# First-stage weight tiles requested two ahead, normed rows of the recurrence requested in two parts, modulation tiles and o-gate blocks at other places

## The chip, the core and the metric

The kernel runs on one core of one Trainium2 chip. The core has five engines, each of which takes its own instructions strictly in order: TensorE (PE in the profile, with its weight loads as PEld), VectorE (DVE), ScalarE (ACT), GpSimd (POOL) and SyncE (SP), which here only issues transfers from HBM. Engines meet through semaphores: an instruction whose input isn't ready holds up everything behind it on its engine.

The metric is the device time of one execution in microseconds (us), as the median of several runs.

## What is computed

A trunk of two layers over 256 positions of width 2048, all in float32. Layer 0 has an mLSTM mixer, layer 1 a gated linear recurrence; each is followed by an MLP with a squared ReLU. Ahead of each of the four parts stands a modulated RMS norm, whose shift, scale and gate come from the vector c through a matrix of 2048 x 6144.

```python
def ada_modulate(x, c, w, b):
    mod = jax.nn.silu(c) @ w + b
    shift, scale, gate = jnp.split(mod, 3, axis=-1)
    h = rms_norm(x) * (1.0 + scale[:, None, :]) + shift[:, None, :]
    return h, gate[:, None, :]

def mlstm_mixer(h, w_in, b_gate, norm_g, w_out):
    proj = h @ w_in                      # q, k, v, o and two gates per head
    ...
    hh = mlstm_chunkwise(q, k, v, li, lf).transpose(0, 2, 1, 3)
    hh = hh * lax.rsqrt(jnp.mean(hh * hh, axis=-1, keepdims=True) + EPS)
    hh = hh.reshape(B, S, V_W) * norm_g.astype(jnp.float32)
    return (hh.astype(h.dtype) * jax.nn.sigmoid(o)) @ w_out

def rglru_mixer(h, w_in, conv_w, conv_b, w_ra, b_ra, w_ri, b_ri, lam, w_out):
    xb, gb = jnp.split(h @ w_in, 2, axis=-1)
    ...                                  # convolution over 4 positions, two gates, scan
    y = hs.astype(h.dtype) * jax.nn.gelu(gb)
    return y @ w_out

# layer 0: x += gate * mlstm(h); x += gate * mlp(h); layer 1: the same with rglru; final norm
```

## The kernel before

**Arithmetic.** Every float32 operand is split into a high and a low part, and a product is made of two or three matmuls. A weight tile of 128 x 2048 (1 MB) arrives as `raw` (four buffers, tag "raw"); `weights()` (lines 158 to 170) requests it on SP's queue (L160) and cuts it into two halves, `whi` on ACT (L167) and `wlo` on DVE (L168), with four buffers of each, so two tiles' worth. An activation row of 128 x 256 is split into a `pair` (ACT L180 or L177, DVE L181 or L178).

**Modulation tiles.** The matrix of the modulations comes as 192 tiles of 1 MB (`adaraw`, requested at L124), each of which DVE multiplies and sums in one instruction (L126). They belong to no particular place: `fill()`, `pace()` and `need()` (lines 134 to 150) lay them down between the weight tiles, at rates set by `QKV_RATE` (per weight tile in the five groups of the first stage) and by `PACE` (how many are to be done by the end of each later stage).

**First stage** (`group()`, lines 472 to 525). The 16 rows of 128 inputs are normed in five groups of 2, 4, 4, 4 and 2; forty weight tiles cover q, k, v and half of the o columns. For each weight tile, `group()` requests it, splits it, and multiplies it into accumulators `mm` in PSUM (L498); groups after the first preload the accumulator with the sum so far (ACT L513), and each accumulator is copied out again (ACT L524). After 34 tiles and the direct first one, and before the last group of five, stands the gate block (`gblk`, L550), which has a weight tile of its own.

**Heads and o-gate blocks** (`mix0`, lines 545 to 755). Eight heads follow, each with scores, state, numerator and denominator (`num`, `den`), mean square (`hss`) and gating. The other half of the o columns is computed in eight o-gate blocks, one weight tile each, that stand between the steps of the heads; the tuple `OB` says where. Its first entry stands ahead of the first scores, entries 1 + 2h and 2 + 2h behind the state and behind the scores of the next head. After every second head two normed, gated rows of `th` are made and split into `zhi` (ACT L718) and `zlo` (DVE L719). The output projection then takes one quad of blocks and twelve single blocks, each of which ends in `residual()` (xall, L329).

**Recurrence** (lines 760 to 864). For n = 0 and 1 the products run on rows that aren't normed yet (`unnormed`) and are corrected afterwards; from n = 2 (`MORE_RG`) on they use the 16 normed rows, made by `modulated()` from `hmod` (DVE L304) and `pair` (ACT L180, DVE L181). All 16 are asked for at n = 2 (lines 796 and 797). Gate products (`gacc`) of each n follow its convolution (`xf`, DVE L805 and L808).

The order on each engine is written out by a scheduler from the program's order, priorities (splits and modulation sums are brought forward) and buffers, so that edits to the program shift rows of several engines.

Of the kernel before, what the change touches and what calls it, by code (L numbers as in the profile page):

```python
# [8 lines left out]
F32 = mybir.dt.float32  # L9
# [6 lines left out]
P = 128  # L16
DM = 2048
S = 256
KC = DM // P
# [22 lines left out]
MORE_RG = 2  # L42
# [6 lines left out]
GROUPS = (2, 4, 4, 4, 2)  # L49
DIRECT = (0,)  # L50
OG = 8

OB = (0, 1, 0, 1, 0, 1, 0, 1, 0, 1, 0, 1, 0, 1, 0, 1, 0)

QKV_RATE = (1.6, 1, 1, 1, 1.2)
PACE = dict(o=54, out0=66, w1a=82, w1b=92, mlp0=168, mix1=170, out1=176, mlp1=192)


@with_exitstack
def trunk_kernel(ctx, tc, xT_d, par_d, ada_d, wqkv_d, wg_d, wo_d, awoa_d, awo_d, bwi_d, bg_d, bwo_d,  # L60
                 w1a_d, w1b_d, bwia_d, w1_d, w2_d, out_d):
    nc = tc.nc
# [5 lines left out]
    wpool = ctx.enter_context(tc.tile_pool(name="wpool", bufs=4))  # L68
# [86 lines left out]
        filler += [(i, 32 + j) for j in range(KC)]  # L155


    def weights(src):
        raw = wpool.tile([P, DM], F32, name="raw", tag="raw")
        nc.sync.dma_start(out=raw, in_=src)  # L160
        out = []
        for i in range(2):
            sl = raw[:, i * HALF:(i + 1) * HALF]
            hi = wpool.tile([P, HALF], F32R, name="whi", tag="whi", bufs=SPLIT_BUFS)
            lo = wpool.tile([P, HALF], F32R, name="wlo", tag="wlo", bufs=SPLIT_BUFS)
            with tc.high_priority(offset=PRIO):
                A.activation(hi, sl, AF.Copy)  # L167
                V.tensor_tensor(out=lo, in0=sl, in1=hi.bitcast(F32), op=ALU.subtract)  # L168
            out.append((hi, lo))
        return out  # L170
# [281 lines left out]
    r = tmp.tile([P, S], F32, name="nrstd", bufs=1)  # L452
    rsqrt(r, ss, 1.0 / DM, EPS)
    hs = []
# [5 lines left out]
    def group_h(gi):  # L460
# [8 lines left out]
            hs.append(p)  # L469
        return h32  # L470

    def group(gi, h32):


        gn, k0 = GROUPS[gi], sum(GROUPS[:gi])
        per = (4096 + OG * P) // 512
        nt = per * k0 // 4
        width = DM // gn
        for nb in range(per * gn // 4):
            direct = nt in DIRECT  # L480
            gh = h32 if direct else [[p[:, 0, :], p[:, 1, :]] for p in hs[k0:k0 + gn]]
            if direct:
                w = wpool.tile([P, DM], F32, name="wdir", tag="raw")
                nc.sync.dma_start(out=w, in_=wqkv_d[nt])
            else:
                w = weights(wqkv_d[nt])
            nt += 1

            def part(kk, o, n):
# [55 lines left out]
    with ExitStack() as mctx:  # L545
# [198 lines left out]
        for kg in range(4):  # L744
            w = weights(awoa_d[kg])
            for kk in range(4):
                hi, lo = w[kk // 2]
                for b in range(4):
                    o = kk % 2 * 512 + b * P
# [10 lines left out]
    with ExitStack() as mctx:  # L760
# [18 lines left out]
        hs = []  # L779
        for n4 in range(4):  # L780
# [5 lines left out]
            for n in range(n4 * 2, n4 * 2 + 2):  # L786
# [6 lines left out]
                    V.tensor_tensor(out=lo, in0=src, in1=hi.bitcast(F32), op=ALU.subtract)  # L793
                    gw.append((hi, lo))
                xf, xp = [], []
                if n == MORE_RG:
                    hs += [modulated(2, j, r) for j in range(KC)]
                for j in (2 * n, 2 * n + 1):
                    if n < MORE_RG:
                        acc, c = scaled(accs[j] if n == 0 else early_block(bwi_d[j], us), r)  # L800
# [13 lines left out]
                for d in range(2):  # L814
                    j = 2 * n + d
# [132 lines left out]
```

## Time and profile before

| | |
|---|---|
| Time, median of 3 runs | 2271.15 us (2270.98 to 2273.05) |
| The profiled execution's own time | 2271.59 us |
| Its span in the profile | 2269.9 us |
| Granted clock of TensorE, mean over the span | 0.99 |
| Read from HBM | 596.93 MB |

A profile is of one execution. Its views: busy time by engine over the span or over chosen windows; groups of instructions by line with the idle time before them; waits (which line of which engine waited for which other); the order in time of each engine's instructions; and transfers. In the rows of the order in time, the first number is the start in us, the second the length, and brackets hold the idle time before it and what released it; "x4" is four instructions in one row. A matmul's listed length reaches past the start of the next one, since they are pipelined. L-numbers are lines of the kernel before.

### The profile page before, as it was taken

The numbers are of one execution on the slowest core, as the hardware profiler recorded it, in microseconds if no ns is written. First come the engines' busy times: TensorE is split into PE (matmuls) and PEld (weight loads), VectorE is DVE, ScalarE is ACT, GpSimd is POOL, SyncE is SP. The second block draws the span as 40 slices with busy tenths as digits, with TensorE's granted clock in tenths as the row PEclk, the third lists the DMA queues.
The fourth block names the chain that finished last, engine by engine and source line by source line (L and its number), as shares of the span: only waits on it lengthen the run. The fifth ranks groups of instructions, "written<-read, shape, count | busy, mean of one in ns | idle before, by whom it ended". The sixth has DMA issues, their size and how long they took to land.

```text
span 2269.9 us, 34176 instructions
## 1 busy us (share of the span) xinstructions
PE 2191.2 (97%) x13606; PEld 1955.9 (86%) x13606; DVE 1719.1 (76%) x2199; ACT 1279.8 (56%) x1997; POOL 84.4 (4%) x70
## 2 busy tenths in 40 slices
PE   7999899999999999999999799999999999999998
PEld 6787799898888888888889799889888888888887
DVE  6777778999998778888888877898875555555554
ACT  5666687445674335555444777756664334665443
POOL 0000000210000000000110000020000000000110
PEclk9999999999999999999999899999999999999999
DMA  8988876989779989898887354676875555555552
GB/s 341 349 315 319 319 263 222 333 305 344 285 288 345 333 327 340 323 336 327 326 327 277 143 195 178 241 260 237 320 277 205 187 187 189 192 191 186 186 186 93
DMA packets 88672, 601.27 MB, mean 265 GB/s; under 512 B 10424, under 2 KB 14648, under 8 KB 16192
## 3 DMA queue, kind: packets, MB, share of 16 engines
q1 hardware_dynamic: 86400, 598.03, 72.5%
q8 instruction: 107, 1.75, 0.3%
q10 hardware_dynamic: 2112, 1.05, 0.2%
q14 instruction: 53, 0.43, 0.0%
HBM read 596.93 MB, written 2.11 MB: 264 GB/s over the span
## 4 chain that ended last, share of the span: by engine, by line
PE 73%; DVE 3%; ACT 1%; issue 1%; DVEq 0%; ACTq 0%
PE mm L193 42%; PE mm L194 22%; PE mm L211 1%; PE mm L210 1%; PE mm L212 1%; PE mm L188 1%; PE mm L187 1%; PE mm L189 1%; DVE wlo L168 1%; DVE adaraw L126 1%; PE mm L350 0%; ACT whi L167 0%; PE gacc L187 0%; PE gacc L188 0%; PE gacc L189 0%
## 5 line engine op out<-in xcount | busy, mean ns | idle before, releaser
L193 PE MATMUL mm<-pair,whi 128*128 128x512 f32 x4272 | 1497.8, 395 | 15.6 <-DVE pair L181 14.9
L194 PE MATMUL mm<-pair,wlo 128*128 128x256 f32 x4272 | 1197.2, 281 | 8.8 <-DVE wlo L168 8.8
L168 DVE TENSOR_TENSOR wlo<-raw,whi 128x1024 fp32r<-128x1024 f32 x736 | 893.7, 1234 | 375.4 <-ACT whi L167 372.0
L167 ACT ACTIVATE whi<-raw 128x1024 fp32r<-128x1024 f32 x736 | 767.2, 1056 | 568.2 <-PE mm L193 420.1
L193 PEld LDWEIGHTS mm<-pair,whi 128*128 128x128 f32 x4272 | 802.8, 188 | 203.9 <-issue 12.3
L194 PEld LDWEIGHTS mm<-pair,wlo 128*128 128x128 f32 x4272 | 804.8, 188 | 12.3 <-DVE wlo L168 11.8
L126 DVE SCALAR_TENSOR_TENSOR adaraw<-adaraw,cbc 128x2050 f32<-128x2050 f32 x192 | 438.3, 2286 | 10.9 <-DMA adaraw<-in_ada 10.7
L498 PE MATMUL mm<-pair,whi 128*128 128x256 f32 x736 | 136.3, 288 | 8.5 <-ACT mm L513 4.6
L329 DVE SCALAR_TENSOR_TENSOR xall<-mm,mod,xall 128x256 f32<-128x256 f32 x170 | 81.4, 482 | 80.3 <-PE mm L194 71.9
L498 PEld LDWEIGHTS mm<-pair,whi 128*128 128x128 f32 x736 | 114.4, 193 | 12.4 <-ACT whi L167 5.7
L188 PE MATMUL mm<-pair,whi 128*128 128x256 f32 x432 | 122.1, 283 | 0.0
L187 PE MATMUL mm<-pair,whi 128*128 128x256 f32 x432 | 121.9, 282 | 0.0
L189 PE MATMUL mm<-pair,wlo 128*128 128x256 f32 x432 | 121.6, 281 | 0.0
L498 PE MATMUL mm<-pair,wlo 128*128 128x256 f32 x368 | 104.0, 291 | 8.1 <-DVE wlo L168 7.8
L371 ACT ACTIVATE hsum<-hsum 128x256 f32<-128x256 f32 x121 | 49.4, 413 | 91.3 <-DVE hsum L254 79.3
L284 POOL TENSOR_TENSOR nacc<-nacc,nsq 128x256 f32<-128x256 f32 x52 | 74.0, 1424 | 346.4 <-ACT nsq L275 339.0
L498 PE MATMUL mm<-whi,pair 128*128 128x512 f32 x256 | 82.0, 396 | 1.0 <-ACT whi L167 0.7
L187 PEld LDWEIGHTS mm<-pair,whi 128*128 128x128 f32 x432 | 81.5, 189 | 0.4
L189 PEld LDWEIGHTS mm<-pair,wlo 128*128 128x128 f32 x432 | 81.6, 189 | 0.2 <-DVE wlo L168 0.2
L188 PEld LDWEIGHTS mm<-pair,whi 128*128 128x128 f32 x432 | 81.5, 189 | 0.0
L498 PEld LDWEIGHTS mm<-pair,wlo 128*128 128x128 f32 x368 | 70.1, 194 | 12.0 <-DVE wlo L168 12.0
L210 PE MATMUL mm<-unnormed,whi 128*128 128x258 f32 x272 | 77.4, 285 | 0.0
(217 smaller groups left out, 2038.4 us busy)
## 6 DMA issues: line engine op xcount, KB each, us to landing
raw<-in_w SPq DMA_DIRECT2D x220, 1024.0 KB, 5.0
adaraw<-in_ada SPq DMA_DIRECT2D x192, 1025.0 KB, 5.6
raw<-in_wqkv SPq DMA_DIRECT2D x39, 1024.0 KB, 7.8
raw<-in_w1a SPq DMA_DIRECT2D x32, 1024.0 KB, 6.2
raw<-in_bwi SPq DMA_DIRECT2D x28, 1024.0 KB, 4.9
raw<-in_bwo SPq DMA_DIRECT2D x16, 1024.0 KB, 4.9
raw<-in_awo SPq DMA_DIRECT2D x12, 1024.0 KB, 5.0
raw<-in_wo SPq DMA_DIRECT2D x8, 1024.0 KB, 8.6
```

The lines of the kernel that those rows point to most:

```text
L126: V.scalar_tensor_tensor(out=raw, in0=raw, scalar=1.0, in1=cbc, op0=ALU.mult, op1=ALU.mult, accum_out=mod[i][:, j:j + 1])
L167: A.activation(hi, sl, AF.Copy)
L168: V.tensor_tensor(out=lo, in0=sl, in1=hi.bitcast(F32), op=ALU.subtract)
L187: PE.matmul(out, lhsT=whi, rhs=hi, start=first, stop=False)
L188: PE.matmul(out, lhsT=whi, rhs=lo, start=False, stop=False)
L189: PE.matmul(out, lhsT=wlo, rhs=hi, start=False, stop=last)
L193: PE.matmul(out, lhsT=whi, rhs=p.rearrange("p a t -> p (a t)"), start=first, stop=False)
L194: PE.matmul(out[:, 0:S], lhsT=wlo, rhs=p[:, 0, :], start=False, stop=last)
L210: PE.matmul(out[:, 0:UX], lhsT=whi, rhs=u[:, 0:UX], start=first, stop=False)
L284: G.tensor_tensor(out=self.acc, in0=self.acc, in1=sq, op=ALU.add)
L329: V.scalar_tensor_tensor(out=xT[j], in0=acc[:, a:a + S], scalar=mod[i][:, 32 + j:33 + j], in1=xT[j], op0=ALU.mult, op1=ALU.add)
L498: PE.matmul(out, lhsT=l, rhs=m, start=clear and kk + n == 0, stop=kk == gn - 1 and n == len(ops) - 1, skip_group_check=True)
```

## The change

Weight tiles of the first stage are requested by `tile_ahead()`, which asks for tiles up to two past the one being used before that one is split; ahead of the gate block it stops at tile 34, in the last group at tile 39. The modulation rates of groups 1 to 4 fall from 1, 1, 1, 1.2 to 0.9, 0.9, 0.9, 1, and four entries of `PACE` change: 51 modulation tiles instead of 54 are done by the end of the heads, 90 instead of 92 by the end of w1b, 162 instead of 168 by the end of the first MLP and 169 instead of 170 by the end of the recurrence. One o-gate block now stands ahead of the first scores, and the one behind the state of the last head is gone. In the recurrence the normed rows 0 to 7 are asked for at n = 0 and the rows 8 to 15 at n = 1. What is computed is the same.

```diff
-OB = (0, 1, 0, 1, 0, 1, 0, 1, 0, 1, 0, 1, 0, 1, 0, 1, 0)
-
-QKV_RATE = (1.6, 1, 1, 1, 1.2)
-PACE = dict(o=54, out0=66, w1a=82, w1b=92, mlp0=168, mix1=170, out1=176, mlp1=192)
+OB = (1, 1, 0, 1, 0, 1, 0, 1, 0, 1, 0, 1, 0, 1, 0, 0, 0)
+
+QKV_RATE = (1.6, 0.9, 0.9, 0.9, 1)
+AHEAD = 2
+PACE = dict(o=51, out0=66, w1a=82, w1b=90, mlp0=162, mix1=169, out1=176, mlp1=192)
...
-    def weights(src):
+    def load(src):
         raw = wpool.tile([P, DM], F32, name="raw", tag="raw")
         nc.sync.dma_start(out=raw, in_=src)
+        return raw
+
+    def weights(src):
+        return split(load(src))
+
+    def split(raw):
         out = []
...
+    raws = []
+
+    def tile_ahead(nt, last):
+
+        while len(raws) <= min(nt + AHEAD, last):
+            raws.append(load(wqkv_d[len(raws)]))
+        return raws[nt]
+
     def group(gi, h32):
...
-            if direct:
-                w = wpool.tile([P, DM], F32, name="wdir", tag="raw")
-                nc.sync.dma_start(out=w, in_=wqkv_d[nt])
-            else:
-                w = weights(wqkv_d[nt])
+            w = tile_ahead(nt, per * (KC if gi == len(GROUPS) - 1 else KC - GROUPS[-1]) // 4 - 1)
+            if not direct:
+                w = split(w)
             nt += 1
...
-                if n == MORE_RG:
-                    hs += [modulated(2, j, r) for j in range(KC)]
+                if n < 2:
+                    hs += [modulated(2, j, r) for j in range(8 * n, 8 * n + 8)]
```

Lines move by up to 13: the split is L174 (ACT) and L175 (DVE) after, the preload L526, the copy-out L537, the modulation sum L127, hmod L311, the row's pair L187 and L188, zlo L732.

**ACT in the first stage.** The rows are in the order of ACT, around weight tiles 8 to 11. `mm<-v4` is a preload, `v0<-mm` a copy-out; qk6 and qk7 are the two accumulators of tile 8, v0 and v1 those of tile 9, v2 and v3 those of tile 10. Before, the split of tile 10 is whi_840 and whi_844:

```order
L513 ACTIVATE mm_891<-v4_199 128x512
L180 ACTIVATE pair_1108<-hmod_1106,mod0_127 128x256
L524 ACTIVATE v0_195<-mm_805 128x512
L513 ACTIVATE mm_906<-v5_200 128x512
L167 ACTIVATE whi_840<-raw_838 128x1024
L167 ACTIVATE whi_844<-raw_838 128x1024
L524 ACTIVATE v1_196<-mm_820 128x512
```

and after it is whi_841 and whi_845:

```order
L537 ACTIVATE qk6_193<-mm_739 128x512
L526 ACTIVATE mm_864<-v3_198 128x512
L174 ACTIVATE whi_841<-raw_729 128x1024
L174 ACTIVATE whi_845<-raw_729 128x1024
L537 ACTIVATE qk7_194<-mm_766 128x512
L526 ACTIVATE mm_892<-v4_199 128x512
L537 ACTIVATE v0_195<-mm_806 128x512
L526 ACTIVATE mm_907<-v5_200 128x512
L174 ACTIVATE whi_884<-raw_796 128x1024
```

Tile 10's split stood behind the copy-out of tile 9's first accumulator (v0) and now stands behind that of tile 8's first (qk6), one tile earlier. The same holds for tiles 7 to 22 and 28 to 30; the splits of tiles 23 to 27 and 31 to 34 stand as before. On PE, the products of a tile's second accumulator, which stood partly between those of its first, now follow the first for tiles 7 to 14, 16 to 22 and 28 to 31.

**DVE behind the last head.** The rows are in the order of DVE, from the mean-square part of heads 6 and 7 (rsu, rs) to their last zlo. `adaraw` is the sum of one modulation tile, `wlo` half a weight tile. Before:

```order
L126 SCALAR_TENSOR_TENSOR adaraw,mod_128<-adaraw,cbc 128x2050
L168 TENSOR_TENSOR wlo<-raw,whi 128x1024 x2
L264 SCALAR_TENSOR_TENSOR rsu<-rs,rsy 128x512
L265 SCALAR_TENSOR_TENSOR rsu<-rsu,rsy 128x512
L168 TENSOR_TENSOR wlo<-raw,whi 128x1024
L266 SCALAR_TENSOR_TENSOR rs<-rsu,rsy 128x512
L126 SCALAR_TENSOR_TENSOR adaraw,mod_128<-adaraw,cbc 128x2050
L714 TENSOR_TENSOR th<-th,rs 128x512 x2
L168 TENSOR_TENSOR wlo<-raw,whi 128x1024
L719 TENSOR_TENSOR zlo<-th,zhi 128x512
L168 TENSOR_TENSOR wlo<-raw,whi 128x1024
L719 TENSOR_TENSOR zlo<-th,zhi 128x512
```

and after:

```order
L271 SCALAR_TENSOR_TENSOR rsu<-rs,rsy 128x512
L127 SCALAR_TENSOR_TENSOR adaraw,mod_128<-adaraw,cbc 128x2050
L272 SCALAR_TENSOR_TENSOR rsu<-rsu,rsy 128x512
L127 SCALAR_TENSOR_TENSOR adaraw,mod_128<-adaraw,cbc 128x2050
L273 SCALAR_TENSOR_TENSOR rs<-rsu,rsy 128x512
L175 TENSOR_TENSOR wlo<-raw,whi 128x1024
L727 TENSOR_TENSOR th<-th,rs 128x512 x2
L127 SCALAR_TENSOR_TENSOR adaraw,mod_128<-adaraw,cbc 128x2050
L732 TENSOR_TENSOR zlo<-th,zhi 128x512
L127 SCALAR_TENSOR_TENSOR adaraw,mod_128<-adaraw,cbc 128x2050
L732 TENSOR_TENSOR zlo<-th,zhi 128x512
```

Four modulation sums now stand between the first rsu and the last zlo where one stood, and one weight half where three stood. On PE, 126 products of other blocks lay between head 7's last den and the first product that reads the zhi made from heads 6 and 7; after the change it is 69. Of the products with the first three weight tiles of the output projection's quad, 124 lay behind that den, and now 33.

**DVE in the recurrence.** The rows are in the order of DVE around the normed rows (hmod, and pair from hmod). Before, they stand behind the second convolution (gb, w and TT belong to the gates and the scan):

```order
L244 TENSOR_TENSOR gb<-mm,nrstd 128x256
L832 SCALAR_TENSOR_TENSOR w_12122<-th,xf 128x256
L246 TENSOR_SCALAR shc<-mm 128x1
L304 SCALAR_TENSOR_TENSOR hmod<-xall,mod_129,nrstd 128x256 x3
L168 TENSOR_TENSOR wlo<-raw,whi 128x1024
L304 SCALAR_TENSOR_TENSOR hmod<-xall,mod_129,nrstd 128x256 x4
```

and after, the first eight follow the norm's factor at once:

```order
L273 SCALAR_TENSOR_TENSOR nrstd<-rsu,rsy 128x256
L311 SCALAR_TENSOR_TENSOR hmod<-xall,mod_129,nrstd 128x256
L175 TENSOR_TENSOR wlo<-raw,whi 128x1024
L188 SCALAR_TENSOR_TENSOR pair<-hmod,mod_129,pair 128x256
L311 SCALAR_TENSOR_TENSOR hmod<-xall,mod_129,nrstd 128x256 x3
L175 TENSOR_TENSOR wlo<-raw,whi 128x1024
L188 SCALAR_TENSOR_TENSOR pair<-hmod,mod_129,pair 128x256 x3
L311 SCALAR_TENSOR_TENSOR hmod<-xall,mod_129,nrstd 128x256 x2
```

The other eight (hmod x1, x5 and x2, then pair x8) stand ahead of the second pair's convolution and behind its predecessor's.

## The prediction

> **What bounds the kernel now.** I read the page's busy times first, then busy time by stretch, then the waits of the stretch that loses most, then the order in time inside it. From the page:
>
> ```profile
> span 2269.9 us, 34176 instructions
> PE 2191.2 (97%) x13606; PEld 1955.9 (86%) x13606; DVE 1719.1 (76%) x2199; ACT 1279.8 (56%) x1997; POOL 84.4 (4%) x70
> raw<-in_wqkv SPq DMA_DIRECT2D x39, 1024.0 KB, 7.8
> ```
>
> TensorE (PE) is busy 97% of the span, so all edits together can win only from the 78.7 us in which it is idle, and a little more where its clock is halved. The views by window say where that idle time lies (start:end, length, PE, weight loads, DVE, ACT, POOL, clock, DMA share, GB/s):
>
> ```profile
> 25.00:85.00 60.00, 54.73 (x328) 47.75 (x328) 46.77 (x50) 37.16 (x60) 0.00 (x0) 0.94 0.91 345
> 85.00:262.00 177.00, 162.35 (x1009) 138.73 (x1009) 132.16 (x127) 113.49 (x168) 0.00 (x0) 1.00 0.87 325
> 417.00:480.00 63.00, 58.75 (x482) 58.34 (x481) 61.92 (x69) 26.77 (x44) 24.12 (x12) 0.97 0.94 348
> 440.00:480.00 40.00, 40.00 (x341) 40.00 (x340) 38.92 (x39) 16.92 (x23) 13.79 (x7) 1.00 0.99 371
> 1222.00:1273.00 51.00, 51.00 (x416) 50.21 (x415) 41.71 (x88) 36.98 (x53) 0.00 (x0) 1.00 0.59 207
> 1273.00:1286.00 13.00, 0.89 (x5) 0.61 (x4) 12.42 (x32) 11.57 (x23) 0.00 (x0) 0.58 0.22 81
> ```
>
> Two places stand out: weight tiles 8 to 34 of the first stage (85 to 262), and one hole of 12 us in the recurrence. In the first, no engine is full: DVE works 132 of 177 us. The waits there, and one tile of it in time:
>
> ```profile
> DVE wlo L168 <- ACT whi L167: 36.9, 28, 2.3
> PE mm L498 <- DVE wlo L168: 13.1, 27, 0.5
> ```
>
> ```profile
> 142.33 0.38 SPq L160 DMA_DIRECT2D raw<-in_wqkv  x1
> ...
> 148.57 0.60 ACT L524 ACTIVATE qk<-mm 128x512 f32<-128x512 f32 x1 [2.23 <-PE mm L498]
> ...
> 149.74 1.99 ACT L167 ACTIVATE whi<-raw 128x1024 fp32r<-128x1024 f32 x2
> ...
> 156.38 2.00 ACT L167 ACTIVATE whi<-raw 128x1024 fp32r<-128x1024 f32 x2
> ...
> 150.83 0.74 PE L498 MATMUL mm<-pair,whi 128*128 128x256 f32 x4 [0.18 <-ACT whi L167]
> 152.09 0.39 PE L498 MATMUL mm<-pair,wlo 128*128 128x256 f32 x1 [0.52 <-DVE wlo L168]
> 152.32 0.40 PE L498 MATMUL mm<-pair,whi 128*128 128x256 f32 x2
> ...
> 157.28 0.28 PE L498 MATMUL mm<-pair,wlo 128*128 128x256 f32 x1
> 157.48 0.73 PE L498 MATMUL mm<-whi,pair 128*128 128x512 f32 x2
> ```
>
> The tile asked for at 142.33 lands, by the page's median of 7.8 us, near 150.1, yet its split starts at 156.38. What holds it is not the transfer: the split of tile n+1 stands on ACT behind the copy-out of tile n's first accumulator (148.57 for the tile before), and ACT itself waits 2.23 us for PE there. DVE's half follows ACT's, and PE waits for both. One tile takes 157.48 − 150.83 = 6.65 us. Undisturbed, 42 products run from 152.32 to 157.28, 0.118 us each, so 48 products need 5.67. Over the stretch it is 177/27 = 6.55 us a tile: **0.88 us lost per tile**. (The busy column hides part of it, since the modelled end of each last product reaches into the gap.)
>
> **The change, part by part.** Sums are made against the profiled execution, 2271.6 us (span 2269.9 and 1.7 around it); the runs' median is 2271.15, the same within 0.02%.
>
> *Two tiles ahead.* By the ACT order, the split of tile n+2 now stands where that of n+1 stood, for tiles 8 to 22 and 28 to 30; for 23 to 27 and 31 to 34 it stands as before. Where it has moved, it is ready a whole tile early and PE should run at 5.67. Tile 31 I count with these, since PE no longer puts products of tile 30's second accumulator into its first and so frees ACT about 1 us sooner. That is 19 of the 27 tiles: 19 × 0.88 = 16.7, **+17** (gains are positive). The cover has to hold elsewhere: DVE per tile is 2 wlo (2.36), 0.9 modulation tile (0.9 × 2.37) and a pair or hmod (0.4), 4.9 of 5.67. DMA has to bring 1.9 tiles of 1.05 MB in 5.67 us, 352 GB/s, against 325 now and 371 in the densest window. From that, 325 kept means 6.13 us a tile and only +8; the other eight tiles freed as well means 27 × 0.88, +23.
>
> *Start, gate block, entry of the heads.* The first tiles' requests now go ahead of modulation tiles on SP's one queue, so the modulated rows of group 1 come later; this queue ran at 345 GB/s, and one modulation tile moved behind a raw tile is 3 us at that rate, of which PE has most covered: **−0.8**. Around the gate block the lookahead stops, so its tile is asked for as late as before, and its split stands behind one more copy-out and two modulation tiles (4.7 us) on DVE. The waits there now:
>
> ```profile
> PE mm L498 <- ACT mm L513: 4.6, 2, 3.4
> PE cp L648 <- ACT kw L630: 2.1, 1, 2.1
> ```
>
> Neither is removed; the first head's state now has one o-gate block ahead of it. Between 0 and −5, I take **−2**. The last group's lookahead reaches the end and has little left to win.
>
> *o-gate blocks and the modulation tiles.* This is where I expect the change to give back. No o-gate block is left behind the last head's state. Now:
>
> ```profile
> 390.02 0.39 PE L664 MATMUL den<-qw,Cn 128*128 128x128 f32 x2
> 391.26 0.42 DVE L668 SCALAR_TENSOR_TENSOR em<-em,ad 128x256 f32<-128x256 f32 x1
> 391.78 2.29 DVE L126 SCALAR_TENSOR_TENSOR adaraw<-adaraw,cbc 128x2050 f32<-128x2050 f32 x1
> 394.00 1.22 DVE L168 TENSOR_TENSOR wlo<-raw,whi 128x1024 fp32r<-128x1024 f32 x1
> 405.49 1.29 DVE L714 TENSOR_TENSOR th<-th,rs 128x512 f32<-128x512 f32 x2
> 406.21 0.63 ACT L718 ACTIVATE zhi<-th 128x512 fp32r<-128x512 f32 x1 [1.88 <-DVE th L714]
> 409.57 0.68 DVE L719 TENSOR_TENSOR zlo<-th,zhi 128x512 fp32r<-128x512 f32 x1
> ```
>
> From the last denominator (390.02 + 0.39 = 390.4) to the end of the first normed, gated row zhi (406.84) pass 16.4 us, since DVE puts three modulation tiles and four weight halves between. Today 126 products lie in between (14.9 us): the wait is 0.5. In the new order only 69 do (8.1 us). The DVE chain has three modulation tiles and three halves, with two more modulation tiles just ahead of it (I take 1.7 us later); zlo then has one more ahead. So PE stops for 8 to 12 us. Does out0 win it back? DVE is full from 391 to 480 (61.92 of 63 in 417 to 480), so it sets the end of out0. Behind em up to out0's end stand 16 modulation tiles and 30 halves before, 18 and 26 after: 2 × 2.37 − 4 × 1.2 = 0, the same load. But em now comes with 91 fewer products still to do (33 of the output projection's first three weight tiles instead of 124), 91 × 0.118 = 10.7 us later in PE's own work, and 1.7 more by the backlog: **−12.4**. Bounds: −5 if DVE's modulation tiles slip behind; −17 if the stop also halves the clock.
>
> That last bound needs a row of its own, taken in the recurrence:
>
> ```profile
> 1285.41 0.77 PE L193 MATMUL mm<-pair,whi 128*128 128x512 f32 x1 [12.11 <-DVE pair L181]
> ...
> 1288.11 0.63 PE L193 MATMUL mm<-pair,whi 128*128 128x512 f32 x1
> 1288.54 0.41 PE L194 MATMUL mm<-pair,wlo 128*128 128x256 f32 x1
> 1288.75 0.45 PE L193 MATMUL mm<-pair,whi 128*128 128x512 f32 x1
> ```
>
> After 12.11 us of waiting PE needs 0.64 us for a pair of products (1288.11 to 1288.75) until 3.3 us have passed: 1.7 us lost beside the wait. The Trainium skill, "TensorE: Matmul & The Clock Gate", section "What's actually happening", says the same: after an idle window of about 3.4 us the array gets half its clock until about 3.4 us of work have gone by. By that rule the new stop on the o-gate would cost 1.7 more, and the sum would be 1.7 us worse; by the DVE row for 417 to 480 that time is paid out of DVE's bound already, and I leave it out.
>
> *Recurrence.* The hole ends at 1285.41. In it DVE makes normed rows (seven of its hmod and four pairs in these groups):
>
> ```profile
> 1274.31 1.27 DVE L304 SCALAR_TENSOR_TENSOR hmod<-xall,mod,nrstd 128x256 f32<-128x256 f32 x3
> 1276.70 1.66 DVE L304 SCALAR_TENSOR_TENSOR hmod<-xall,mod,nrstd 128x256 f32<-128x256 f32 x4
> 1284.79 1.67 DVE L181 SCALAR_TENSOR_TENSOR pair<-hmod,mod,pair 128x256 fp32r<-128x256 f32 x4
> ```
>
> A row costs DVE 0.42 + 0.42, sixteen rows 13.4 us. From 1222 to 1273 DVE has 51.00 − 41.71 = 9.3 us free, and the new order puts eight rows (6.7 us) early there. The other eight stand ahead of the second pair's convolution: DVE is then 13.4 − 9.3 = 4.1 us behind, and I add 1.7 for the gate products that now find their operands late; 5.8 us of waiting remain of 12.1. With 1.7 of half clock gone: 12.1 − 5.8 + 1.7 = **+8**. Ends: +1 if DVE's free time, spent waiting for ACT's halves, can't be used; +11 if nothing remains.
>
> *Modulation tiles of the first MLP.* Four fewer stand there and five more in the recurrence, 2.37 us each on DVE, which is busy 76% of the span and has 9.3 us free in the recurrence's first part alone: 0, with ±2 for both ends.
>
> Sum: −0.8 + 17 − 2 − 12.4 + 8 = +9.8, so 2271.6 − 9.8 = **2261.8, rounded to 2262 us**.
>
> **The rivals.**
>
> 1. *The stop behind the last head stays hidden.* If DVE has run its modulation tiles ahead under the earlier o-gate blocks and isn't the bound of out0, the term is about −1. Against: DVE's own rows fill nearly all of the 16.4 us, and only 8.1 us of products lie over them. Time: 2271.6 − (9.8 + 11.4) = 2250.4.
> 2. *DMA sets the pace of the first stage.* At 325 GB/s the tile takes 6.13 us: 19 × 0.42 = 8 rather than 17, sum +0.8, 2270.8: no change. For: 0.87 share at 325 now. Against: 371 in 440 to 480, 345 from 25 to 85.
> 3. *Slower.* The same mechanism further on: a tile with 0.9 modulation tile is 1.99 MB. At 300 GB/s it needs 6.63 us, more than the 6.55 it takes now, −1.5 in all, and the sum is −8.7: 2280.3. The change turns slower by over 4.5 us when the nineteen tiles gain under 2.7 us, 0.14 each, so at 6.41 us a tile or 310 GB/s. For: requests queued two ahead compete with modulation tiles that DVE still has to free. Against: the two rows just named.
> 4. *The change doesn't do what it says.* The gap per tile stays since the split halves have no more buffers than before. Then 17 becomes 0: 2278.8. Against: in 85 to 262 ACT's split never waits for PE to free a half; it waits behind the copy-out. The Trainium skill, "Perfetto Trace Analysis", section "Optimization Strategy", speaks for it: the same gap repeating on the engine that should be saturated can mean too few buffers for the next tile. The change adds none. By the trace's order at 149.74 and 156.38 it doesn't apply.
>
> **How the numbers follow.** Forecast 0.50 (2255 to 2268 by its terms' bounds, likeliest 2262); rival 1 0.18; rival 2 0.20; rival 3 0.07; rival 4 0.05. A measurement of this kernel tells about 0.2%, 4.5 us, from no change: faster is below 2266.6, slower above 2275.7. Faster: 0.18 and most of 0.50, with a little of rival 2: 0.67. Slower: 0.12. Same: 0.21. For 8 in 10 the range keeps the forecast, rival 2 and most of rival 1, and leaves out rivals 3 and 4 and the far end of rival 1: 2248 to 2275.
>
> **What would show it.** Right: from tile 8 to the gate block about 160 us where it is 177 now, with steps of 5.7 between tiles and single steps of 6.5 near tiles 23 to 27 and 32 to 34; a PE wait for zhi or zlo of 8 to 12 us after the last denominator; in the recurrence two or three waits of 2 to 4 us instead of one of 12.1, with the clock near full. Wrong: waits of ACT's split for raw tiles in the first stage (rivals 2 and 3), steps of 6.5 throughout (rival 4), or PE full behind the last head (rival 1). The o-gate term is the one I trust least: it rests on DVE being full up to 480.

## The result: 2243.4 us, nearly three times the forecast gain

| | Before | After |
|---|---|---|
| Time, median of 4 runs each | 2271.07 us (2269.70 to 2273.05) | 2243.40 us (2241.30 to 2244.50) |
| Profiled execution | 2271.59 us | 2244.50 us |
| Its span | 2269.9 us | 2242.8 us |

The ratio is 0.9876 (95% interval 0.9859 to 0.9894): 27.7 us were won. The forecast was 2262, a gain of 9.8 from the profiled execution, with 2248 to 2275 as the range. The direction was right and the size was not.

The page of the changed kernel, for the lines that were shown of the one before:

```profile
span 2242.8 us, 34191 instructions
PE 2181.7 (97%) x13606; PEld 1960.5 (87%) x13606; DVE 1722.3 (77%) x2199; ACT 1286.1 (57%) x1997; POOL 90.1 (4%) x70
```

The same 13606 products, 9.5 us less PE busy time and 17.6 us less idle time. (Busy time falls too, because the modelled end of a product that stands ahead of a gap reaches into the gap.) To see where the time went, one compares the same points of the work in both traces, not the same times. The points below are read from the order in time; a positive number is time won up to there or in that part.

| Point of the work | Before, us | After, us | Won so far | In this part: measured | Forecast |
|---|---|---|---|---|---|
| gate block's first product | 261.90 | 245.28 | 16.6 | +16.6 | +16.2 (17 − 0.8) |
| first state product (cp) | 315.32 | 298.14 | 17.2 | +0.6 | −2 |
| last den of the last head, with equal work done | 401.1 | 384.90 | 16.2 | −1.0 | 0 |
| last residual of the output projection | 488.19 | 488.74 | −0.6 | −16.8 | −12.4 |
| last residual of the first MLP | 1219.62 | 1209.97 | 9.7 | +10.2 | 0 |
| last residual of the recurrence's projection | 1536.46 | 1511.03 | 25.4 | +15.8 | +8 |
| last product | 2261.37 | 2234.26 | 27.1 | +1.7 | 0 |

(At the last den the changed kernel has done 91 more products of the output projection. 390.41 + 91 × 0.118 = 401.1 is the time at which the kernel before is as far. Ahead of the gate block's first product the changed kernel has a wait of 1.74 us, for that block's own split; at the product before it 18.5 us are won.)

The sum of the first stage came out as forecast. Three other terms did not: what was lost behind the last head, the MLP, and the recurrence. The windows of the changed kernel over the stretches that were shown before, or that correspond to them:

```profile
85.00:245.00 160.00, 155.65 (x1015) 140.03 (x1013) 124.23 (x121) 114.69 (x168) 0.00 (x0) 1.00 0.85 322
385.00:489.00 104.00, 88.46 (x668) 86.82 (x667) 95.16 (x109) 42.04 (x68) 25.53 (x14) 0.90 0.90 328
400.00:410.00 10.00, 6.91 (x30) 6.61 (x31) 7.36 (x10) 2.33 (x4) 0.00 (x0) 0.52 0.92 327
489.00:1210.00 721.00, 718.07 (x4198) 631.77 (x4197) 619.20 (x759) 376.78 (x578) 21.05 (x14) 1.00 0.88 316
1210.00:1262.00 52.00, 51.76 (x419) 51.12 (x418) 47.11 (x103) 39.48 (x63) 0.00 (x0) 1.00 0.59 205
1262.00:1275.00 13.00, 13.00 (x82) 11.38 (x82) 12.91 (x25) 10.23 (x17) 0.00 (x0) 1.00 0.69 238
```

Up to the gate block PE idles 4.4 us in 160, against 14.7 in 177 before. The recurrence is full: DVE works 47.11 of 52 us in its first part where it worked 41.71 of 51 before, and no hole follows. Behind the last head stands a new stop. It shows in the order in time of PE (start, length, and in brackets the wait and what ended it):

```profile
391.94 0.39 PE L196 MATMUL mm<-zhi,wlo 128*128 128x256 f32 x1 [1.82 <-DVE wlo L175]
...
401.77 1.43 PE L194 MATMUL mm<-zhi,whi 128*128 128x256 f32 x5 [5.55 <-ACT zhi L731]
404.53 0.58 PE L195 MATMUL mm<-zlo,whi 128*128 128x256 f32 x1 [1.32 <-DVE zlo L732]
...
435.28 0.58 PE L196 MATMUL mm<-zhi,wlo 128*128 128x256 f32 x1 [4.06 <-DVE wlo L175]
```

Between the last head and the first residual PE waits 5.55 + 1.32 = 6.9 us for zhi and zlo, a little under the 8 to 12 that were forecast for them, and 8.7 us with the wait for wlo. The clock is at 0.52 from 400 to 410. The wait of 4.06 at 435 us was there before too (4.18).

### The profile page after: what moved, and what is told of

Read it like the earlier page. It is cut to its first block, busy times and chain, and to the rows that moved or that the text cites. A ratio compares the mean times of both kernels' runs of the same rounds, so it can differ in the third digit from the quotient of the medians.

```text
span 2242.8 us, 34191 instructions
## 1 busy us (share of the span) xinstructions
PE 2181.7 (97%) x13606; PEld 1960.5 (87%) x13606; DVE 1722.3 (77%) x2199; ACT 1286.1 (57%) x1997; POOL 90.1 (4%) x70
## 3 DMA queue, kind: packets, MB, share of 16 engines
q8 instruction: 106, 1.74, 0.3%
## 4 chain that ended last, share of the span: by engine, by line
PE 86%; DVE 7%; ACT 3%; issue 2%; DMA 1%; SPq 0%; DVEq 0%; ACTq 0%
PE mm L200 42%; PE mm L201 22%; PE mm L511 8%; DVE wlo L175 3%; PE mm L196 2%; PE mm L195 2%; PE mm L194 2%; DVE adaraw L127 2%; ACT whi L174 1%; PE mm L218 1%; PE mm L217 1%; PE mm L219 1%; DMA adaraw<-in_ada 1%; PE mm L357 0%; DVE hmod L311 0%
## 5 line engine op out<-in xcount | busy, mean ns | idle before, releaser
L175 DVE TENSOR_TENSOR wlo<-raw,whi 128x1024 fp32r<-128x1024 f32 x736 | 900.2, 1233 | 380.1 <-ACT whi L174 375.9
L174 ACT ACTIVATE whi<-raw 128x1024 fp32r<-128x1024 f32 x736 | 771.9, 1057 | 609.7 <-PE mm L200 476.7
L201 PEld LDWEIGHTS mm<-pair,wlo 128*128 128x128 f32 x4272 | 804.7, 188 | 1.7 <-DVE wlo L175 1.1
L127 DVE SCALAR_TENSOR_TENSOR adaraw<-adaraw,cbc 128x2050 f32<-128x2050 f32 x192 | 439.7, 2291 | 50.7 <-DMA adaraw<-in_ada 41.7
L511 PE MATMUL mm<-pair,whi 128*128 128x256 f32 x736 | 136.0, 288 | 10.7 <-ACT pair L187 5.7
L196 PE MATMUL mm<-zhi,wlo 128*128 128x256 f32 x256 | 75.8, 296 | 6.6 <-DVE wlo L175 6.6
L194 PE MATMUL mm<-zhi,whi 128*128 128x256 f32 x256 | 74.9, 297 | 7.6 <-ACT zhi L731 5.5
L196 PEld LDWEIGHTS mm<-pair,wlo 128*128 128x128 f32 x432 | 81.8, 189 | 0.0
```

Source lines behind the costliest of these rows:

```text
L127: V.scalar_tensor_tensor(out=raw, in0=raw, scalar=1.0, in1=cbc, op0=ALU.mult, op1=ALU.mult, accum_out=mod[i][:, j:j + 1])
L194: PE.matmul(out, lhsT=whi, rhs=hi, start=first, stop=False)
L196: PE.matmul(out, lhsT=wlo, rhs=hi, start=False, stop=last)
L201: PE.matmul(out[:, 0:S], lhsT=wlo, rhs=p[:, 0, :], start=False, stop=last)
L511: PE.matmul(out, lhsT=l, rhs=m, start=clear and kk + n == 0, stop=kk == gn - 1 and n == len(ops) - 1, skip_group_check=True)
```

## The experiments

Each kernel below was run beside the kernel before, four timed runs of its own. Times are medians; the ratio is to the kernel before, with its 95% interval.

### The recurrence: rows at n = 2 again

```diff
-                if n < 2:
-                    hs += [modulated(2, j, r) for j in range(8 * n, 8 * n + 8)]
+                if n == MORE_RG:
+                    hs += [modulated(2, j, r) for j in range(KC)]
```

> The changed kernel with one part undone: all 16 normed rows of the recurrence are asked for at n = 2 again. Theory: the recurrence gained 14 to 16 us because of the rows' place alone (the 12.1 us wait, its 1.7 us of half clock, and small waits behind it), so 2243 becomes 2257 to 2260 and one wait of about 12 us for a pair is back. Rival: the place of the rows is worth the 8 us that the prediction gave it and the rest came from the modulation tiles that were moved out of and into this stage: 2251, with a wait under 8 us.

2261.8 us, ratio 0.9953 (0.9938 to 0.9968), a little beyond the theory's range. The hole is back, in the order in time of PE and in the window around it:

```profile
1274.42 0.77 PE L200 MATMUL mm<-pair,whi 128*128 128x512 f32 x1 [12.45 <-DVE pair L188]
```

```profile
1262.00:1275.00 13.00, 0.57 (x2) 0.51 (x3) 13.00 (x34) 11.52 (x22) 0.00 (x0) 0.64 0.47 161
```

From the last residual of the MLP to the last product this kernel takes 1041.4 us, the changed one 1024.3: the place of the rows is worth **17.2 us**, 16.0 of them up to the last residual of the recurrence's projection, and that is all of the recurrence's gain. The forecast had 8.

### The recurrence: all rows at n = 1

```diff
-                if n < 2:
-                    hs += [modulated(2, j, r) for j in range(8 * n, 8 * n + 8)]
+                if n == 1:
+                    hs += [modulated(2, j, r) for j in range(KC)]
```

> The changed kernel with all 16 normed rows asked for at n = 1, none at n = 0. Theory: work that nobody on PE waits for (the scan and gating of the first pair and the second pair's convolution, some 14 us of DVE) is what the rows push back, so their 13.4 us cost PE little wherever they stand ahead of the first product that reads them: 2243 to 2247. Rival, the prediction's sum: DVE has 9.3 us free there in all and is behind by the rest, so that a wait of 4 to 9 us comes back in front of the first normed product: 2248 to 2255.

2256.3 us, 0.9929 (0.9914 to 0.9944): the rival is nearer, a little beyond its range. From the MLP's last residual on it is 1032.3 us, 8.0 more than the changed kernel. The other 5.6 of the profiled execution were lost ahead of that, where PE, DVE and ACT have the same order of instructions in both kernels. So they are no effect of the edit that the order shows. Executions of the same order differ by a few us at one point: the first state product came at 298.14 us after the change, at 296.45 with the rows at n = 2, and at 300.30 here, where the wait ahead of it was 3.3 us instead of 2.2 and the clock stood at 0.50 from 300 to 305 us instead of 0.86. Small differences at one point of one trace say little for that reason. The wait in front of the first normed products:

```profile
1267.56 0.47 PE L200 MATMUL mm<-pair,whi 128*128 128x512 f32 x1 [1.62 <-ACT pair L187]
1268.60 0.58 PE L201 MATMUL mm<-pair,wlo 128*128 128x256 f32 x1 [0.57 <-DVE wlo L175]
```

So sixteen rows at one place still cost something, 2.2 us of listed waits here and 8 in all, and my theory that they cost nothing anywhere fell. The step that the forecast got wrong is narrower: with eight rows at n = 0 and eight at n = 1 PE has no listed wait for a normed row.

### The first MLP: its modulation rates undone

```diff
-PACE = dict(o=51, out0=66, w1a=82, w1b=90, mlp0=162, mix1=169, out1=176, mlp1=192)
+PACE = dict(o=51, out0=66, w1a=82, w1b=92, mlp0=168, mix1=170, out1=176, mlp1=192)
```

> The changed kernel with PACE of w1b, mlp0 and mix1 put back to 92, 168 and 170. Theory: the first MLP gained 10 us because 72 modulation tiles instead of 76 stand in it, so that no weight half waits behind two of them on DVE; undone, 2243 becomes 2252 to 2254 and the waits of 0.6 to 1.5 us for wlo between 580 and 1170 us are back. Rival: the waits went because the stages before it ended otherwise, and the rates do nothing: 2243 to 2245.

2257.3 us, 0.9930 (0.9913 to 0.9946), a little more than expected. The time from the last residual of the output projection to that of the MLP goes from 721.2 to 732.0 us; 2.4 of these 10.8 are lost near 500 us, where the order is still the same in both kernels. The lists of waits, first of this kernel (491 to 1223 us), then of the kernel before (490 to 1219):

```profile
PE mm L201 <- DVE wlo L175: 6.5, 6, 1.5
...
PE mm L200 <- DVE pair L188: 2.9, 3, 2.0
```

```profile
PE mm L194 <- DVE wlo L168: 7.0, 7, 1.5
...
PE mm L193 <- DVE pair L181: 2.7, 3, 1.3
```

The changed kernel has only the waits for pairs there (2.9 us). What made the waits for wlo can be read in the kernel before, around one of them (808.89 us):

```profile
799.25 2.29 DVE L126 SCALAR_TENSOR_TENSOR adaraw<-adaraw,cbc 128x2050 f32<-128x2050 f32 x1
...
801.46 2.29 DVE L126 SCALAR_TENSOR_TENSOR adaraw<-adaraw,cbc 128x2050 f32<-128x2050 f32 x1
...
807.22 0.48 DVE L329 SCALAR_TENSOR_TENSOR xall<-mm,mod,xall 128x256 f32<-128x256 f32 x1 [3.46 <-PE mm L194]
807.62 2.35 DVE L168 TENSOR_TENSOR wlo<-raw,whi 128x1024 fp32r<-128x1024 f32 x2
```

```profile
801.93 2.01 ACT L167 ACTIVATE whi<-raw 128x1024 fp32r<-128x1024 f32 x2 [4.97 <-DMA raw<-in_w]
...
808.89 0.38 PE L194 MATMUL mm<-pair,wlo 128*128 128x256 f32 x1 [1.48 <-DVE wlo L168]
```

Two modulation tiles stand side by side, and ACT waits 4.97 us for a weight tile to land (801.93). Then `wlo` stands behind xall, which waits 3.46 us for PE's last product of the block: as in the first stage, a half that PE needs next is queued behind a read-out of what PE does now, and PE waits for it, 1.48 us. The other two waits of 1.48 us in that stretch (1082.61 and 1162.87) show the same rows, with one short row between the two tiles. Three more waits (916.83, 945.68 and 1024.86 us; 0.76, 0.62 and 0.62 us) show a single modulation tile at a bad place. The first of them:

```profile
911.48 2.29 DVE L126 SCALAR_TENSOR_TENSOR adaraw<-adaraw,cbc 128x2050 f32<-128x2050 f32 x1
...
914.15 0.42 ACT L371 ACTIVATE hsum<-hsum 128x256 f32<-128x256 f32 x1 [3.04 <-DVE hsum L254]
...
915.55 2.36 DVE L168 TENSOR_TENSOR wlo<-raw,whi 128x1024 fp32r<-128x1024 f32 x2 [1.43 <-ACT whi L167]
```

The tile stands ahead of the read-out `hsum` on DVE, ACT waits 3.04 us for that read-out, and the split stands behind it on ACT, so both halves come late.

Compared product by product, the kernel with the rates undone falls behind the changed one by 8.4 us in six steps of 0.9 to 1.8 us, each at its counterpart of one of these six waits, and hardly anywhere else after 625 us, where the two orders part. So the old rates, and with them the places of the modulation tiles, cost these 8.4 us. DVE runs 97 modulation tiles in this stretch before, 94 with the rates undone and 88 after. Two of them stand side by side 8 times before, 8 times with the rates undone, and not once after; but seven of the eight have no listed wait of PE behind them, so a pair alone doesn't make a wait. DVE is idle for much of that time: the count of its free microseconds, on which I had put this term at 0, is not what decides here. (What the trace doesn't explain of the 13.9 us between the medians I have not followed.)

### The first stage: requests ahead, and rates, each alone

```diff
-AHEAD = 2
+AHEAD = 0
```

> The changed kernel with AHEAD = 0: each weight tile of the first stage is asked for when it is split, all else as changed. Theory: the first stage takes some 16 us longer and little of it is made up later, since what the stage behind the heads gave back (17 us) belongs to the o-gate blocks and the modulation tiles there: 2255 to 2259. Rival: the end of the output projection (488.2 us before, 488.7 after) is set by something that runs through from the start, such as the sum of the bytes, so a later first stage costs nothing there: 2243 to 2246, with the end of the output projection still near 488 us.

2243.3 us, 0.9871 (0.9856 to 0.9886): the rival, and no difference from the changed kernel. The gate block starts at 250.4 (5.1 us later), the output projection ends at 486.6 (2.1 us earlier). Undoing the rates instead:

```diff
-QKV_RATE = (1.6, 0.9, 0.9, 0.9, 1)
+QKV_RATE = (1.6, 1, 1, 1, 1.2)
```

> The changed kernel with QKV_RATE put back to 1.6, 1, 1, 1, 1.2; weight tiles are still asked for two ahead. Theory: the gate block starts 16.6 us earlier after the change, of which 11.5 were left without the requests ahead, so the lower rate moved the splits on ACT and the requests ahead are worth 5 to 7; with the old rates the gate block starts at 254 to 257 us (245.3 after, 261.9 before), and the time is 2249 to 2255. Rival, the one of the prediction: the requests ahead make the gain, the gate block starts near 245 to 247 and the time is 2241 to 2245.

2251.4 us, 0.9904 (0.9888 to 0.9921), as the theory had it. So the requests ahead moved the smaller part of the splits on ACT. In ACT's order of each kernel one can count, among tiles 8 to 34, the splits that stand at least one tile early, and set beside it what is won up to the last product ahead of the gate block, and that block's first product:

```
kernel                              early splits   won ahead of it   per split   gate block starts
before                                    0                                          261.90
requests ahead, old rates                 7              7.16          1.02          256.59
rates 0.9, no requests ahead             11             11.52          1.05          250.39
the change: both                         18             18.52          1.03          245.28
```

An early split is worth 1.0 us in all three, a little more than the 0.88 of the forecast, and it is won where the split is early: with the requests ahead alone PE is 6.8 us ahead at 152 us, behind the last of its seven early splits, and 6.85 us at 206. The two kernels with requests ahead then wait 1.7 us for the gate block's split, the others don't. The cause was put down to the wrong edit. With one modulation tile for each weight tile, a split stays behind the same copy-out for good once it has fallen there. With 0.9 there is a place now and then where two weight tiles are asked for with none between, and from it the split runs early for three or four tiles. The requests ahead give the same once, at the start, for seven; with both it is fifteen in a row.

### Behind the last head: modulation tiles

```diff
-PACE = dict(o=51, out0=66, w1a=82, w1b=90, mlp0=162, mix1=169, out1=176, mlp1=192)
+PACE = dict(o=54, out0=66, w1a=82, w1b=90, mlp0=162, mix1=169, out1=176, mlp1=192)
```

> The changed kernel with PACE o = 54 instead of 51: three more modulation tiles before the end of the heads. By the instruction order DVE then has 13 modulation tiles instead of 18 between the last head and the end of the output projection, and 2 instead of 3 between the last denominator and the last normed rows; PE has 15 more products over that chain. Theory: DVE's load sets the end of the output projection, so up to 5 x 2.37 = 12 us are won: 2232 to 2236. Rival 1: only the chain behind the last head counts, 2.4 + 1.8 us: 2239 to 2240. Rival 2: the bytes set that end: 2243.

**2232.4 us**, 0.9824 (0.9809 to 0.9838), as the theory had it: three modulation tiles put elsewhere are worth 11 us. Groups of DVE's instructions from the last head to the end of the output projection (busy, mean ns, idle before), first after the change (385 to 489 us), then with 54 (385 to 476.5):

```profile
L127 DVE SCALAR_TENSOR_TENSOR adaraw<-adaraw,cbc 128x2050 f32<-128x2050 f32 x20 | 46.1, 2312 | 0.0
```

```profile
L127 DVE SCALAR_TENSOR_TENSOR adaraw<-adaraw,cbc 128x2050 f32<-128x2050 f32 x14 | 31.9, 2284 | 0.0
```

Six tiles and 14 us less on DVE, and the output projection ends 12.6 us earlier (476.09 for 488.74). With o = 60:

```diff
-PACE = dict(o=51, out0=66, w1a=82, w1b=90, mlp0=162, mix1=169, out1=176, mlp1=192)
+PACE = dict(o=60, out0=66, w1a=82, w1b=90, mlp0=162, mix1=169, out1=176, mlp1=192)
```

> The changed kernel with PACE o = 60: nine more modulation tiles before the end of the heads than after the change, six more than in the run with 54. By the order DVE has 8 of them behind the last head instead of 18 (13 with 54). Theory: 5 x 2.37 - 2 x 1.2 = 9.5 us less than with 54 on DVE, but PE is then the bound with some 11 us left to win, and the heads have 87 - 72 = 15 us of DVE to spare for nine tiles of 2.37: 2224 to 2230. Rival: the heads become the place that is bound by DVE, and what is won behind them is lost in them: 2232 to 2238.

2231.9 us, 0.9822 (0.9807 to 0.9837): the rival, at its lower end. Behind the last head PE is now all but full (1.4 us of waits up to the end of the output projection), yet its last den comes at 389.7 instead of 384.8, with waits like this one among the heads:

```profile
333.00 0.38 PE L196 MATMUL mm<-pair,wlo 128*128 128x256 f32 x1 [1.65 <-DVE wlo L175]
```

### Behind the last head: the o-gate blocks

```diff
-OB = (1, 1, 0, 1, 0, 1, 0, 1, 0, 1, 0, 1, 0, 1, 0, 0, 0)
+OB = (0, 1, 0, 1, 0, 1, 0, 1, 0, 1, 0, 1, 0, 1, 0, 1, 0)
```

> The changed kernel with the o-gate blocks where they stood before. By the order 125 products lie over the last head's chain (71 after the change), 88 more products are left behind it, and DVE has 22 modulation tiles and 29 weight halves up to the end of the output projection instead of 18 and 26. Theory: DVE's load sets that end: 10.4 us are won by the earlier chain, 4 x 2.37 + 3 x 1.2 = 13.1 lost: 2244 to 2248. Rival: the waits for zhi and zlo behind the last head (6.8 us) and their half clock are the cost, and go: 2230 to 2236.

2251.9 us, 0.9911 (0.9896 to 0.9926). That excludes the rival (2230 to 2236), which blamed the visible waits; it is beyond the theory's range too. The waits for zhi are gone, and others stand in their place: PE waits for `whi` four times, 11.2 us in all, and ACT for weight tiles to land:

```profile
PE mm L194 <- ACT whi L174: 11.2, 4, 4.4
ACT whi L174 <- DMA raw<-in_awo: 9.3, 2, 8.0
```

DVE has 22 modulation tiles to run there; I read the late weight tiles as the same load with another face, which no run shows by itself. The same edit, on the kernel with o = 54, where the load is nearly equal:

> The run with PACE o = 54, with the o-gate blocks where they stood before. By the order the load of DVE behind the last head is then nearly that of the run with 54 (13 modulation tiles and 29 halves against 13 and 27), and 97 products instead of 86 lie over the chain. Theory: with the load equal, the place of the o-gate blocks decides only by those 11 products (1.3 us) and two halves (2.4 us), so 2231 to 2236. Rival 1: a block ahead of the first scores is worth much by itself (the run with the old places at 51 was 8.5 us slower): 2238 to 2243. Rival 2: the missing block behind the last head costs some 7 us of waiting: 2224 to 2227.

2237.0 us, 0.9851 (0.9836 to 0.9866), between the theory and its first rival; the output projection ends at 476.9 us, against 476.1. Against 0.9824 (0.9809 to 0.9838) the new places are a little better or equal; that the last block's absence costs, as the prediction had it, is excluded (2224 to 2227 expected then).

### Less binding: toward a faster version

Three more edits of numbers, the first two on the kernel with o = 54:

```diff
-AHEAD = 2
+AHEAD = 0
```

> The run with PACE o = 54, with AHEAD = 0. 11 of the tiles 8 to 34 then have their split one tile earlier in ACT's order, instead of 18. Theory: the first stage loses about 5 us, as with 51; with 51 the loss vanished because DVE's load set the end of the output projection, and with 54 it is close to setting it still, so between 0 and 5 us are lost: 2233 to 2237, with the gate block at 250 us. Rival: what is lost in the first stage is lost in full, 2237 to 2239.

2236.3 us, 0.9846 (0.9831 to 0.9861): the gate block starts at 249.2, 3.4 us later than with o = 54 alone, and 3.9 us are lost, though the intervals still overlap a little. With less on DVE behind the last head, the requests ahead seem worth what they win.

```diff
-QKV_RATE = (1.6, 0.9, 0.9, 0.9, 1)
+QKV_RATE = (1.6, 0.8, 0.8, 0.8, 1)
```

> The run with PACE o = 54, with QKV_RATE 1.6, 0.8, 0.8, 0.8, 1. By ACT's order all 27 tiles from 8 to 34 then have the early split, against 18 with 0.9, 11 without the requests ahead, 7 with the old rates and 0 before. The start of the gate block has followed that count: 245.3, 250.4, 256.6 and 261.9 us, about 0.9 us a tile. Theory: nine more tiles, 8 us, the gate block starts at 237 to 238; the modulation tiles left out (three) fall to the heads, so 2224 to 2229. Rival: the transfers bind once the stall is gone, the gate block stays above 242, and the time at 2230 to 2234.

2230.8 us, 0.9823 (0.9808 to 0.9837): the rival in the time, something between in the first stage. The gate block starts at 241.35, 4.5 us earlier, not 8. But the stall of the split is gone from all tiles, and no wait for a transfer is listed from 85 us to the gate block. A new wait has come, at the first product of a group, for that group's modulated rows, whose own modulation tiles are now late:

```profile
131.39 0.91 PE L511 MATMUL mm<-pair,whi 128*128 128x256 f32 x5 [1.24 <-ACT pair L187]
...
189.38 0.91 PE L511 MATMUL mm<-pair,whi 128*128 128x256 f32 x5 [1.26 <-ACT pair L187]
```

and behind the last head the wait for zhi and zlo is 3.26 + 1.90 us again, since the tiles that were left out come there.

```diff
-QKV_RATE = (1.6, 0.9, 0.9, 0.9, 1)
+QKV_RATE = (1.6, 0.85, 0.85, 0.85, 1)
...
-PACE = dict(o=51, out0=66, w1a=82, w1b=90, mlp0=162, mix1=169, out1=176, mlp1=192)
+PACE = dict(o=56, out0=66, w1a=82, w1b=90, mlp0=162, mix1=169, out1=176, mlp1=192)
```

> The changed kernel with QKV_RATE 1.6, 0.85, 0.85, 0.85, 1 and PACE o = 56. 26 tiles have the early split; DVE has 13 modulation tiles behind the last head and one ahead of the last normed rows, with 113 products over that chain. Theory: gate block at 238 to 239 us, waits behind the last head under 2 us, 2220 to 2227. Rival: the heads are bound by DVE (as with 60): 2229 to 2233.

**2223.5 us**, 0.9788 (0.9772 to 0.9804), the best of all: 47.5 us under the kernel before and 20 under the change. 26 of 27 splits are early, the gate block starts at 239.65, one of the two waits for the group's rows is left, and behind the last head PE waits little:

```profile
130.76 0.50 PE L511 MATMUL mm<-pair,whi 128*128 128x256 f32 x2 [1.24 <-ACT pair L187]
...
390.56 0.38 PE L195 MATMUL mm<-zlo,whi 128*128 128x256 f32 x1 [1.22 <-DVE zlo L732]
```

## Why the prediction was off, step by step

**Two tiles ahead, +17: the sum about right, the cause wrong.** The start and the stretch up to the gate block were to win 16.2 and won 18.5 up to the last product ahead of that block, about 1.0 us for each of the 18 tiles whose split stands early. "Two tiles ahead" was the wrong name for it: without the requests ahead, 11.5 of the 18.5 stay, and without the lower rates only 7.2. The forecast read the order of the changed kernel, which holds both edits, and gave the result to the edit that sounded like it; that the sum still came out near is luck as far as the cause goes. Rival 4, that the gap is a lack of buffers, is excluded: with the same raw tiles and halves the gap goes from all tiles at 0.8. The rule of the Trainium skill that was set beside it ("Perfetto Trace Analysis", "Optimization Strategy") therefore doesn't apply to this gap; it came from a place in an in-order queue. Rivals 2 and 3, transfers as the bound, are excluded for this stretch: at 322 GB/s PE idles only 4.4 us.

**Gate block and heads, −2: −2.3.** Counted from the last product ahead of the gate block (18.5 won) to the last den (16.2 won). The split that was seen to stand later is the new wait of 1.74 us. The wait for the preload, in two parts of 3.40 and 1.24 before, is now one of 4.8, the first state's wait 2.24 (2.05 before). A term of this size is within what executions of the same order differ by, so its closeness shows little.

**o-gate blocks and modulation tiles, −12.4: −16.8.** The stop came near the forecast size, and so did the first part of the sum: em starts 2.28 us after the last den where it started 0.85 after it, 1.4 later in place of 1.7, and 10.7 for the 91 products. DVE's load behind em is the same, as forecast. The step that failed is that DVE would be full there. From em to the last residual, before and after:

```profile
391.26:488.19 96.93, 91.82 (x751) 90.73 (x751) 92.31 (x105) 44.30 (x70) 25.62 (x14) 0.98 0.92 337
387.18:488.74 101.56, 86.02 (x652) 84.64 (x651) 92.72 (x107) 40.69 (x65) 25.53 (x14) 0.90 0.90 326
```

DVE idles 8.8 us instead of 4.6, and that is nearly all of the missing 4.4. Its longest idle stretch there, and what ACT waits for:

```profile
408.99 1.06 ACT L174 ACTIVATE whi<-raw 128x1024 fp32r<-128x1024 f32 x1 [6.58 <-PE mm L195]
410.08 1.23 DVE L175 TENSOR_TENSOR wlo<-raw,whi 128x1024 fp32r<-128x1024 f32 x1 [2.72 <-ACT whi L174]
```

ACT's split waits for PE, which runs at half clock then, and DVE waits 2.72 us for the split. So the half clock, left out on the ground that DVE paid for it, was probably not free. With the 1.7 that the Trainium skill's rule on it ("TensorE: Matmul & The Clock Gate", "What's actually happening") was said to add, the term would have been −14.1 and nearer. (How much of the idle time is the half clock's, and how much the stop's, no run separates.) What was wrong outright is the name of the culprit: the o-gate blocks. With them at their old places the kernel is slower, and at nearly equal load the two places differ by less than 1 us at the end of the output projection. With 54 instead of 51 in PACE 12.6 of the 16.8 us come back; the forecast had counted that edit as a part of the term only.

**Modulation tiles of the first MLP, 0: +10.2.** This is the step that failed outright. I asked whether DVE has room for the tiles, and it has. What decides is where they stand: at the old rates some of them, singly or in pairs, bring a weight tile's half late, behind a read-out or behind a split that waited for one, and PE waits for the half, up to 1.5 us, six times. Undone, the rates give these waits back, and 8.4 us with them. The waits for wlo in that stretch were in the trace of before, 7.0 us in seven waits; the prediction's idle time by stretch left out 480 to 1235, and so neither the waits nor the tiles that go were put beside each other. The prediction counted four fewer tiles there; the rates take six from the MLP, and the traces have nine fewer.

**Recurrence, +8: 16 to 17.** The place of the rows is the cause, by 17.2 us. The mis-sized term is the 5.8 us of waiting that were to remain: 0.7 remained, and none of it for a normed row. Without the 5.8, the forecast's own sum gives 12.1 + 1.7 = 13.8 (its bound of +11 for that case was too low), and product by product 14.4 are won across the hole. Another 1.4 or so goes at 1458.5 us, where the kernel before waits 1.27 us for a wlo and the changed one doesn't. The sum let DVE be behind by all that its 9.3 free microseconds could not hold. But the eight rows at n = 1 push back work for which no product waits at that point, the scan and gating of the first pair and the second pair's convolution; that is how I read the order. Put all sixteen there and it is no longer free (8.0 us): the even split matters.

The range missed because each of its ends moved one term and left the others as forecast. Here two terms came out some 8 to 10 us better than priced, one from zero and one from half, and the 4 us by which a third was worse didn't make up for them.

## What to carry to other kernels

Where filler work (here the modulation tiles) is spread among transfers, its rate can decide apart from the load it adds: here at one per weight tile a late split stayed late for good, at a little under one it recovered, and a filler at a bad place, alone or two in a row, made a half of the next weight tile late for the engine that needs it. When several edits share one instruction order, an order tells what all of them do together, and only undoing one at a time tells which did it. And a stretch whose listed waits are small in each case but many should be added up before an edit to its rates is priced at zero.

## What the runs showed of the hardware that I had not expected

After waits of 5.55 and 1.32 us with 1.43 us of products between, the clock was at 0.52 over ten microseconds (400 to 410), of which 5.5 lie behind the second wait (404.53 on). The kernel before was back at full clock 3.3 us after its wait of 12.11 us. Work of about a microsecond between two waits did not bring the clock back; why it took longer than 3.3 us after the second wait isn't shown.
